# Second layer's hyena filter chain moved from the first token mixer to the first layer's last four experts

## The chip, the core and the metric

The kernel runs on one core of a Trainium2 chip. The metric is device time in microseconds (us) of one launch. Engines are called by the names of the profile: PE (TensorE matmuls), DVE (VectorE), ACT (ScalarE), POOL (GpSimd), SP (the queue that issues nearly all DMAs).

## What is computed

Two layers run over 256 context tokens and 256 latent tokens of width 1024. Each layer has a token mixer with four branches and then an expert-choice mixture of 16 experts. One of the branches is a Hyena long convolution. Its filters depend on weights alone, not on the tokens, so a layer's filters may be computed at any time before that layer's convolution:

```python
def hyena_filters(L, p):
    ...
    h = jnp.sin(p['hy_freq'][0] * (feats @ p['hy_w1'] + p['hy_b1']))
    h = jnp.sin(p['hy_freq'][1] * (h @ p['hy_w2'] + p['hy_b2']))
    h = (h @ p['hy_w3']).astype(jnp.float32)
    h = h * (jnp.exp(-dist[:, None] * jnp.abs(p['hy_decay'])) + HY_SHIFT)
    h = h / jnp.sum(jnp.abs(h), axis=0, keepdims=True)
    return h.reshape(L, HY_ORDER, HY_WIDTH)
```

The expert part reads 12 MB of weights per expert and layer (`w1`, `w3`, `w2`, each 1024x1024 in fp32) for 32 tokens per stream.

## The kernel before

The 256 filter positions are sines of sines. On the chip one layer's filters are a **chain** (`chain(l, hp)` inside `hyena_filters`): a 64x256 matmul, seven DVE operations that reduce the argument of the sine, a Sin on ACT, the same again, two 128x512 matmuls, a decay window (Abs, two Exp on ACT and a multiply-add on DVE), column sums by eight 128x1 matmuls, a reciprocal, four transposes, a scaling on DVE, and eight 128x512 matmuls with a DFT matrix `df`. The result is copied out of PSUM in four pieces (`A.activation(Hs[f](), p, AF.Copy)`) and each piece goes to DRAM with a DMA on SP (L775), where the layer's convolution fetches it much later with one DMA on POOL. The four pieces have a buffer each (`Hs`, four of them).

`hyena_filters` is called once, in the first layer's mixer, after the column blocks of GLA and before its `scan`. It runs `chain(0, ...)`, issues the loads of the second layer's small weights (`load_hy(1)`, L1749 to L1751), runs `chain(1, ...)`, and frees its memory. Everything of the chain lives in a region that is open for that time alone.

The mixer around it is a long row of PE work: column blocks (`pd`, tiles of 128x512), steps of the adaLN projection (`pa`, each waits for a 512 KB weight DMA), and the scan (`ps`, 64x64 products, level by level, with DVE and ACT work between levels).

`moe` comes after the mixer. `ffn(e)` takes eight 1 MB weight tiles for `w1` and `w3`, multiplies, applies Silu (ACT, L1636) and a product (DVE), transposes, takes four tiles of `w2`, multiplies, and copies out (`evac`, ACT L1687 and DVE L1685). Weight tiles sit in 19 slots; SP issues each when its slot is free and when the transfer eight places before it has landed, since eight completion semaphores are used in turn. Every four experts `gather` builds the tokens of the next group (`xg`, in the memory of `raws`) and `scatter` adds the last group's outputs (PE `pm`, DVE L1698). After expert 10 the last gather is done; `raws` and the transposed tokens `pre.xt` are then idle until the second layer's weights are reloaded at expert 15.

The order of instructions on each engine is fixed when the program is built, by a scheduler that may lift an instruction over others of its engine. Each engine, SP too, then works its row strictly in that order: an instruction that waits holds all behind it.

Of the kernel before, what the change touches and what calls it, by code (L numbers as in the profile page):

```python
# [51 lines left out]
HY = Pack()  # L52
# [301 lines left out]
def build(tc, ins, outT, dbg=None, stop=None):  # L354
# [66 lines left out]
    def early(name, off=0, **kw):  # L421
        o, c = C0.at[name]
        return c0(o + off, n=kw.pop("n", c - off), **kw)
# [298 lines left out]
    def hyena_filters(hps, df, rb):  # L722

        w, dec, h, ab = (rb.take(n) for n in (1024, 512, 1024, 1024))
        Hs = [rb.take(512) for _ in range(4)]
        def chain(l, hp):
            def hc(name, off=0, n=None, np_=64):
                o, c = HY.at[name]
                return hp(o + off, n=c if n is None else n, np_=np_)

            MAGIC = 12582912.0
            prev = early("feats", np_=33)
            for i, (wn, bn, fn, kdim) in enumerate((("w1", "b1", "f0", 33), ("w2", "b2", "f1", 64))):
                p = ps("s")
                mm(p[0:64, 0:256], hc(wn, np_=kdim), prev, True, True)
                a, k, g = (w(256 * q, n=256, np_=64) for q in (0, 1, 2 + i))
                V.tensor_scalar(a, p[0:64, 0:256], hc(bn), hc(fn), op0=OP.add, op1=OP.mult)
                V.tensor_scalar(k, a, 1.0 / (2 * math.pi), MAGIC, op0=OP.mult, op1=OP.add)
                V.tensor_scalar(k, k, MAGIC, None, op0=OP.subtract)
                c1 = 6.28125  # L740
                c2 = float(np.float32(2 * math.pi - c1))
                c3 = 2 * math.pi - c1 - c2
                for c in (c1, c2, c3):
                    V.scalar_tensor_tensor(a, k, -c, a, op0=OP.mult, op1=OP.add)
                V.tensor_scalar(a, a, 3.1415925, -3.1415925, op0=OP.min, op1=OP.max)
                A.activation(g, a, AF.Sin)
                prev = g
            A.activation(dec(), hp(HY.n, n=512), AF.Abs)
            pa = ps("s")
            for tb in range(2):  # L750
                p = ps("s")
                mm(p, w(768 + tb * 128, n=128, np_=64), hc("w3"), True, True)
# [4 lines left out]
            for q in range(4):  # L757
                for tb in range(2):
                    mm(pa[:, q:q + 1], ab(tb * 512 + q * 128, n=128), cs("ones", n=1), tb == 0, tb == 1)
# [1055 lines left out]
```

## Time and profile before

| | us |
|---|---|
| median of the runs | 1999.94 (1998.57 to 2007.31, three runs) |
| the profiled execution | 2006.5 |
| its span, first to last instruction | 2004.7 |
| PE busy | 1843.2 (92%) |
| DVE / ACT busy | 854.7 (43%) / 529.9 (26%) |

The page's picture in 40 slices of 50 us each shows the stages (a digit is the busy share in tenths, the last row GB/s moved by DMA):

```profile
PE   7999999999999899999897799999998999987877
DVE  5355658798743222221121345869865021110101
DMA  8641122364545999999999855333578999999999
GB/s 312 223 140 58 64 85 78 107 236 136 194 156 218 353 399 350 387 409 409 409 409 409 302 189 180 117 106 137 200 262 336 409 409 409 409 409 409 409 409 332
```

The first layer's mixer ends near 650 us, its experts near 1125 us, the second mixer near 1535 us; the rest is the second layer's experts. In the mixers PE is full and DMA is not; in the experts DMA stands at 409 GB/s for hundreds of us. The chain of the second layer lies between 71 and 121 us, in slices 2 and 3.

### The profile page before, as it was taken

The numbers are of one execution on the slowest core, as the hardware profiler recorded it, in microseconds if no ns is written. First come the engines' busy times: TensorE is split into PE (matmuls) and PEld (weight loads), VectorE is DVE, ScalarE is ACT, GpSimd is POOL, SyncE is SP. The second block draws the span as 40 slices with busy tenths as digits, with TensorE's granted clock in tenths as the row PEclk, the third lists the DMA queues.
The fourth block names the chain that finished last, engine by engine and source line by source line (L and its number), as shares of the span: only waits on it lengthen the run. The fifth ranks groups of instructions, "written<-read, shape, count | busy, mean of one in ns | idle before, by whom it ended". The sixth has DMA issues, their size and how long they took to land.

```text
span 2004.7 us, 28151 instructions
## 1 busy us (share of the span) xinstructions
PE 1843.2 (92%) x11524; PEld 1087.6 (54%) x11524; DVE 854.7 (43%) x1855; ACT 529.9 (26%) x932; POOL 27.9 (1%) x52
## 2 busy tenths in 40 slices
PE   7999999999999899999897799999998999987877
PEld 3667778877887443434232356788997333221213
DVE  5355658798743222221121345869865021110101
ACT  4433447522233110101000243447443000000000
POOL 0000000000000000000000010010000000000000
PEclk9989999999999899999999999999998999999999
DMA  8641122364545999999999855333578999999999
GB/s 312 223 140 58 64 85 78 107 236 136 194 156 218 353 399 350 387 409 409 409 409 409 302 189 180 117 106 137 200 262 336 409 409 409 409 409 409 409 409 332
DMA packets 154148, 550.07 MB, mean 274 GB/s; under 512 B 11042, under 2 KB 22690, under 8 KB 153124
## 3 DMA queue, kind: packets, MB, share of 16 engines
q1 hardware_dynamic: 153444, 545.13, 71.7%
q0 software_dynamic: 576, 3.15, 0.5%
q8 instruction: 91, 1.49, 0.3%
q14 instruction: 37, 0.30, 0.0%
HBM read 545.08 MB, written 3.15 MB: 273 GB/s over the span
## 4 chain that ended last, share of the span: by engine, by line
PE 69%; DMA 19%; DVE 7%; issue 3%; ACT 3%; SPq 0%; DVEq 0%; ACTq 0%
PE pd L431 40%; PE ps L431 15%; DMA base<-moe_w 8%; PE pm L431 7%; DMA r<-moe_w 6%; PE pa L431 4%; DMA base<-ada_w 2%; PE pm L428 1%; DMA base<-wg 1%; DVE base L527 1%; DVE r L844 1%; ACT r L843 1%; PE ps L1640 1%; DMA base<-cb 0%; DVE r L1236 0%
## 5 line engine op out<-in xcount | busy, mean ns | idle before, releaser
L431 PE MATMUL pd<-r 128*128 128x256 f32 (+3 forms) x2976 | 574.4, 364 | 12.9 <-DMA r<-moe_w 6.5
L431 PEld LDWEIGHTS pd<-r 128*128 128x128 f32 (+2 forms) x2976 | 427.3, 184 | 131.4 <-issue 53.8
L431 PE MATMUL pd<-r,r 128*128 128x512 f32 (+3 forms) x1304 | 282.6, 433 | 13.4 <-DMA r<-moe_w 10.8
L431 PEld LDWEIGHTS pd<-r,r 128*128 128x128 f32 (+2 forms) x1304 | 161.8, 166 | 105.0 <-issue 54.8
L844 DVE TENSOR_TENSOR r<-base,r 128x1024 fp32r<-128x1024 f32 x136 | 165.9, 1222 | 110.4 <-ACT r L843 110.0
L843 ACT ACTIVATE r<-base 128x1024 fp32r<-128x1024 f32 x136 | 143.4, 1058 | 252.2 <-PE pd L431 181.2
L431 PE MATMUL ps<-base 32*64 32x64 f32 (+12 forms) x2372 | 177.2, 279 | 15.1 <-DMA base<-hy 5.1
L431 PE MATMUL pd<-r,base 128*32 128x512 f32 (+1 forms) x680 | 166.5, 598 | 11.3 <-DMA r<-moe_w 10.6
L431 PEld LDWEIGHTS ps<-base 32*64 32x64 f32 (+7 forms) x2372 | 112.6, 142 | 76.3 <-issue 42.7
L431 PE MATMUL pm<-base 128*128 128x128 f32 (+12 forms) x660 | 106.1, 327 | 17.5 <-DVE base L1571 5.8
L431 PE MATMUL ps<-r,base 128*64 128x512 f32 (+4 forms) x468 | 98.6, 525 | 12.9 <-DVE base L1641 6.3
L431 PE MATMUL pd<-base 128*32 128x512 f32 (+1 forms) x408 | 100.5, 595 | 6.4 <-DMA base<-moe_w 5.6
L431 PEld LDWEIGHTS pm<-base 128*128 128x128 f32 (+5 forms) x660 | 72.8, 180 | 60.9 <-issue 33.6
L431 PEld LDWEIGHTS pd<-r,base 128*32 128x32 f32 (+1 forms) x680 | 42.0, 122 | 111.2 <-issue 76.4
L1637 DVE TENSOR_TENSOR r<-base,pd 64x512 f32<-64x512 f32 x16 | 10.9, 679 | 214.3 <-PE pd L431 214.3
L1637 DVE TENSOR_TENSOR base<-base,pd 128x512 f32<-128x512 f32 x16 | 11.0, 688 | 190.1 <-PE pd L431 155.9
L1636 ACT ACTIVATE base<-pd 128x512 f32<-128x512 f32 (+1 forms) x32 | 19.0, 594 | 251.1 <-PE pd L431 251.1
L431 PE MATMUL pa<-r,r 128*128 128x512 f32 (+1 forms) x384 | 82.4, 342 | 1.1 <-DVE base L905 1.1
L1687 ACT ACTIVATE base<-ps 32x512 f32<-32x512 f32 (+2 forms) x28 | 14.7, 525 | 251.6 <-PE ps L431 247.2
L1687 ACT ACTIVATE r<-ps 32x512 f32<-32x512 f32 (+2 forms) x32 | 15.3, 480 | 246.2 <-PE ps L431 240.3
L431 PE MATMUL pd<-base,r 128*32 128x512 f32 (+1 forms) x296 | 71.3, 597 | 9.3 <-DMA base<-moe_w 9.3
L1685 DVE COPY r<-ps 32x512 f32<-32x512 f32 (+2 forms) x32 | 17.8, 555 | 123.3 <-ACT r L1687 123.2
(246 smaller groups left out, 1728.8 us busy)
## 6 DMA issues: line engine op xcount, KB each, us to landing
r<-moe_w SPq DMA_DIRECT2D x251, 1024.0 KB, 18.1
base<-moe_w SPq DMA_DIRECT2D x131, 1024.0 KB, 17.4
base<-wg SPq DMA_DIRECT2D x152, 512.0 KB, 3.6
base<-ada_w SPq DMA_DIRECT2D x60, 512.0 KB, 4.7
base<-ada_t SPq DMA_DIRECT2D x24, 512.0 KB, 3.3
r<-ada_w SPq DMA_DIRECT2D x12, 512.0 KB, 10.2
base<-xT SPq DMA_DIRECT2D x4, 1024.0 KB, 6.8
filters<-r SPq DMA_DIRECT2D x8, 256.0 KB, 4.0
```

What stands on the lines that cost most here:

```text
L428: T.transpose(out, in_, ident)
L431: return T.matmul(out, lhsT, rhs, start=start, stop=stop, **kw)
L527: V.tensor_tensor_reduce(self.junk() if s == 0 else b(), b(), self.cb(s * 1024, n=1024), 1.0, cs("adab", l * 48 + c * 8 + j, n=1), OP.mult ...
L843: A.activation(w[0](), raw(), AF.Copy)
L844: V.tensor_tensor(w[1](), raw(), F(w[0]()), op=OP.subtract)
L1636: A.activation(s_(np_=rows), pa[0:rows, :], AF.Silu)
L1637: V.tensor_tensor(h_(np_=rows), s_(np_=rows), pb[0:rows, :], op=OP.mult)
L1640: T.transpose(p[:, q * rows:q * rows + rows], h_(q * 128, n=128, np_=rows), cs("ident", n=rows, np_=rows))
L1685: V.tensor_copy(dst, src)
L1687: A.activation(dst, src, AF.Copy)
```

## The change

`chain` becomes the whole of `hyena_filters(l, hp, c_, df, w, dec, h, ab, Hs)`, with its memory handed in. The first layer's call stays where it was. The second layer's call moves to the front of expert 12 of the first layer's `moe` (`next_filters`). There the working buffers are views of `pre.xt`, and the inputs (the small weights, the sine features `c_`, the DFT matrix `df`) are loaded anew into views of `raws`. Since `pre.xt` has no more room, there is one output buffer `Hs` instead of four.

```diff
-        chain(0, hps[0])
-        load_hy(1)
-        chain(1, hps[1])
...
+            A.activation(Hs[f % len(Hs)](), p, AF.Copy)
+            S.dma_start(out=Hd[l][:, f * 512:f * 512 + 512], in_=Hs[f % len(Hs)]())
...
+        def next_filters():
+
+            t, r = pre.xt, Buf(mem, raws[0].at, 3072)
+            hp, df, c_ = view(r, 0, HY.n + 1024), view(r, HY.n + 1024, 1024), view(r, HY.n + 2048, C0.n)
+            load_hy(1, hp)
+            S.dma_start(out=c_(n=258), in_=ins["c0"][:, 0:258])
+            S.dma_start(out=df(), in_=ins["df"][:, 0:1024])
+            hyena_filters(1, hp, c_, df, view(t, 0, 1024), view(t, 1024, 512), view(t, 1536, 1024), view(t, 2560, 1024),
+                          [view(t, 3584, 512)])
+
         nxt, spare = [], []
         gather(0)
         for gr in range(4):
             for j in range(4):
+                if not last and 4 * gr + j == 12:
+                    next_filters()
                 ffn(4 * gr + j)
...
-    hps = [mem.take(HY.n + 1024) for _ in range(2)]
+    hp0 = mem.take(HY.n + 1024)
...
+    def filters(r):
+        bs = [r.take(n) for n in (1024, 512, 1024, 1024)]
+        Hs = [r.take(512) for _ in range(4)]
+        hyena_filters(0, hp0, c0, df, *bs, Hs)
+        for b in bs + Hs + [hp0, df, c0]:
+            b.free()
```

Line numbers shift: the matmuls and the expert's weight DMAs are L431 and L1614 before, L431 and L1611 after; the store of a filter piece is L775 before and L778 after.

**SP between expert 11 and expert 13.** Before, the row from the last tiles of expert 11 holds weights alone:

```order
L1614 DMA r7_4871<-moe_w3 128x2x1024 x2
L1614 DMA r7_4871<-moe_w2 128x2x1024 x4
L1614 DMA r6_4867<-moe_w1 128x2x1024 x3
L1614 DMA base_58<-moe_w1 128x2x1024
L1614 DMA base_58<-moe_w3 128x2x1024 x3
L1614 DMA r7_4871<-moe_w3 128x2x1024
L1614 DMA r7_4871<-moe_w2 128x2x1024 x4
L1614 DMA r7_4871<-moe_w1 128x2x1024
```

After, it reads:

```order
L1611 DMA r7_4798<-moe_w2 128x2x1024 x4
L724 DMA base_58<-hy 64x644
L725 DMA base_58<-hyr 128x512
L726 DMA base_58<-hyr 1x512
L1729 DMA base_58<-c0 128x258
L1730 DMA base_58<-df 128x1024
L1611 DMA r6_4794<-moe_w1 128x2x1024 x3
L1611 DMA base_58<-moe_w1 128x2x1024
L1611 DMA base_58<-moe_w3 128x2x1024 x3
L1611 DMA r7_4798<-moe_w3 128x2x1024
L1611 DMA r7_4798<-moe_w2 128x2x1024
L778 DMA filters1_62<-base_58 128x512
```

Five loads have come in after expert 11's `w2`; nine weight tiles of expert 12 follow, then the first filter store. Behind that, the last three tiles of expert 12 and the other three stores stand in turn (tile, store, tile, store, tile, store), and only then the first tile of expert 13.

**PE at the scatter before expert 12 and in expert 12** (`pm` is the scatter; `pd422` and `pd423` are expert 12's `w1` and `w3`; `ps413` before is expert 11's `w2`, `ps412` to `ps421` after are the chain). Before:

```order
L431 MATMUL ps413_6225<-r7_4871,base_58 64x512 x16
L431 MATMUL pm414_6246<-r6_4867,base_58 128x256
L431 MATMUL pm415_6251<-r6_4867,base_58 128x256
L431 MATMUL pm414_6246<-r6_4867,base_58 128x256
L431 MATMUL pm415_6251<-r6_4867,base_58 128x256
L431 MATMUL pd422_6294<-r6_4867 64x512 x3
L431 MATMUL pm416_6256<-r6_4867,base_58 128x256 x2
L431 MATMUL pm417_6261<-r6_4867,base_58 128x256 x2
L431 MATMUL pd422_6294<-r6_4867 64x512 x2
```

After, from the second half of the scatter on (the first matmul of the chain, `ps412`, stands four scatter rows further ahead):

```order
L431 MATMUL pm409_6198<-r6_4794,base_58 128x256 x2
L431 MATMUL pm410_6203<-r6_4794,base_58 128x256 x2
L431 MATMUL pd422_6296<-r6_4794 64x512 x2
L431 MATMUL pm411_6208<-r6_4794,base_58 128x256 x2
L431 MATMUL pd422_6296<-r6_4794 64x512 x8
L431 MATMUL ps413_6228<-base_58 64x256
L431 MATMUL pd422_6296<-r6_4794 64x512
L431 MATMUL pd422_6296<-base_58,r6_4794 64x512 x4
L431 MATMUL ps415_6240<-base_58 128x512
L431 MATMUL ps416_6245<-base_58 128x512
L431 MATMUL pd423_6297<-base_58,r6_4794 64x512
L431 MATMUL ps414_6239<-base_58 128x1
```

The chain's matmuls have come in among those of the scatter and of expert 12; the last of them, `ps421`, stands behind the seventh of the sixteen matmuls of `w3`.

**PE in the first mixer.** Before, between the end of the first chain (`ps26`) and the scan (`ps37`, `ps38`, ...), the second chain (`ps27` to `ps36`) is spread over column blocks and projection steps; its first part reads:

```order
L431 MATMUL ps26_596<-r4_530,base_58 128x512 x2
L431 MATMUL ps27_604<-base_58 64x256
L431 MATMUL pa45_762<-base_58 32x256 x8
L431 MATMUL pd78_1153<-r2_227,r3_231 128x512 x13
L431 MATMUL pa45_762<-base_58 32x256 x4
L431 MATMUL pd78_1153<-r2_227,r3_231 128x512 x8
L431 MATMUL ps28_614<-r4_530,base_58 64x256
```

After, the scan (`ps27`, `ps28`, ...) follows the first chain at once, and the same column block (now `pd68`) stands between its levels:

```order
L431 MATMUL ps26_596<-r4_530,base_58 128x512 x2
L431 MATMUL ps27_607<-base_58 64x64 x8
L431 MATMUL ps28_617<-base_58 64x64 x8
L431 MATMUL pa35_689<-base_58 32x256
L431 MATMUL ps29_627<-base_58 64x64 x8
L431 MATMUL ps30_637<-base_58 64x64 x8
```

The column blocks that stood beside the second chain now stand in the scan and after it; the expert slots have the same number and places in memory as before.

## Rows read from the trace of the kernel before

**Rows 1.** Windows: us, busy us of each engine, PE clock, DMA share, GB/s.

```profile
300.00:400.00 100.00, 99.70 (x514) 79.83 (x514) 82.75 (x220) 64.80 (x133) 0.69 (x1) 1.00 0.26 90
85.00:119.20 34.20, 30.73 (x145) 17.71 (x144) 12.46 (x24) 8.73 (x13) 0.31 (x1) 0.90 0.55 178
119.00:158.00 39.00, 37.22 (x653) 27.30 (x652) 29.83 (x61) 14.20 (x28) 2.17 (x4) 0.94 0.39 124
1000.00:1050.00 50.00, 45.72 (x200) 17.26 (x198) 11.02 (x22) 3.54 (x6) 0.31 (x1) 1.00 1.03 409
1050.00:1100.00 50.00, 38.03 (x166) 10.55 (x164) 4.27 (x7) 2.36 (x4) 0.00 (x0) 1.00 1.03 409
```

**Rows 2.** Timeline of PE, 85 to 119 us: start, us, what, idle before.

```profile
85.14 0.64 PE L431 MATMUL ps<-base 33*64 33x256 f32 x2
...
92.88 0.64 PE L431 MATMUL ps<-r,base 64*64 64x256 f32 x2
...
97.30 0.64 PE L431 MATMUL pa<-base 128*32 128x256 f32 x8 [1.38 <-DMA base<-ada_w]
...
99.69 1.98 PE L431 MATMUL ps<-base,r 64*128 64x512 f32 x4
...
102.50 0.28 PE L431 MATMUL ps<-base,r 128*128 128x1 f32 x2
104.03 0.64 PE L431 MATMUL pa<-base 128*32 128x256 f32 x8 [1.25 <-DMA base<-ada_w]
...
105.17 2.37 PE L431 MATMUL ps<-base,r 128*128 128x1 f32 x14
...
109.26 1.05 PE L428 MATMUL ps<-base,r 128*128 128x128 f32 x4
...
111.82 7.45 PE L431 MATMUL ps<-r,base 128*128 128x512 f32 x16
```

**Rows 3.** Timeline of DVE in the same stretch, the second chain.

```profile
93.56 0.53 DVE L737 TENSOR_SCALAR r<-ps,base 64x256 f32<-64x256 f32 x1 [3.46 <-PE ps L431]
...
96.13 0.29 DVE L745 TENSOR_SCALAR r<-r 64x256 f32<-64x256 f32 x1
100.84 0.69 DVE L755 SCALAR_TENSOR_TENSOR r<-r,ps 128x512 f32<-128x512 f32 x1 [4.43 <-PE ps L431]
...
110.42 1.28 DVE L768 TENSOR_TENSOR r<-r,ps 128x512 f32<-128x512 f32 x2 [2.20 <-PE ps L428]
...
112.76 0.67 DVE L769 TENSOR_TENSOR r<-r,base 1x512 f32<-1x512 f32 x1
```

**Rows 4.** Timeline of ACT: a table load, an Abs and a filter copy of the chain.

```profile
74.48 1.28 ACT L754 ACT_TABLE_LOAD   x1
...
102.48 0.63 ACT L756 ACTIVATE r<-r 128x512 f32<-128x512 f32 x1 [0.23 <-DVE r L755]
...
115.87 0.60 ACT L774 ACTIVATE r<-ps 128x512 f32<-128x512 f32 x1 [9.49 <-PE ps L431]
```

**Rows 5.** Timeline of SP at the second chain's four stores.

```profile
116.49 4.43 SPq L775 DMA_DIRECT2D filters<-r  x4
```

**Rows 6.** The page's DMA issues: KB each, median us from issue to landing.

```profile
r<-moe_w SPq DMA_DIRECT2D x251, 1024.0 KB, 18.1
```

**Rows 7.** Timeline of PE at the end of expert 11 and in expert 13.

```profile
994.90 1.94 PE L431 MATMUL pd<-r,base 128*64 128x512 f32 x8 [0.61 <-DMA r<-moe_w]
...
1005.14 1.94 PE L431 MATMUL ps<-r,base 128*64 128x512 f32 x8 [0.63 <-DMA r<-moe_w]
1007.76 1.99 PE L431 MATMUL pm<-r,base 128*128 128x256 f32 x8 [0.68 <-ACT base L1687]
...
1046.07 1.94 PE L431 MATMUL pd<-r 128*64 128x512 f32 x8 [0.62 <-DMA r<-moe_w]
```

**Rows 8.** Timeline of DVE: the last four of the sixteen scatter operations.

```profile
1018.58 1.74 DVE L1698 SCALAR_TENSOR_TENSOR base<-pm,base 128x256 f32<-128x256 f32 x4 [1.19 <-PE pm L431]
```

**Rows 9.** The stores of the filters (L775) by source line.

```profile
DMA to landing us min/median/max: 2.3/4.0/6.3
```

More of the change, by code (lines that the diff above doesn't have):

```diff
@@ L419, in sp, with early @@
         return sm(o + off, dims, **kw)
-    def early(name, off=0, **kw):
+    def early(b, name, off=0, **kw):
         o, c = C0.at[name]
-        return c0(o + off, n=kw.pop("n", c - off), **kw)
+        return b(o + off, n=kw.pop("n", c - off), **kw)
     ident = cs("ident")
@@ L719, in split @@
         V.tensor_tensor(lo, src, F(hi), op=OP.subtract)
[L722 to L749, printed above, removed]
-            for tb in range(2):
-                p = ps("s")
-                mm(p, w(768 + tb * 128, n=128, np_=64), hc("w3"), True, True)
-                ht, at = h(tb * 512, n=512), ab(tb * 512, n=512)
-                A.activation(at, dec(), AF.Exp, scale=early("ndist", tb, n=1))
-                V.scalar_tensor_tensor(ht, at, 0.05, p, op0=OP.add, op1=OP.mult)
-                A.activation(at, ht, AF.Abs)
-            for q in range(4):
-                for tb in range(2):
-                    mm(pa[:, q:q + 1], ab(tb * 512 + q * 128, n=128), cs("ones", n=1), tb == 0, tb == 1)
-            rec = mem.take(4)
-            V.reciprocal(rec(n=4), pa[:, 0:4])
-            V.tensor_copy(dec(0, [[128, 4], [1, 128]]), rec(0, [[1, 4], [0, 128]]))
-            rec.free()
-            pa = ps("s")
-            for q in range(4):
-                tr(pa[:, q * 128:q * 128 + 128], dec(q * 128, n=128))
-            for tb in range(2):
-                V.tensor_tensor(h(tb * 512, n=512), h(tb * 512, n=512), pa, op=OP.mult)
-            V.tensor_tensor(h(512, n=512, np_=1), h(512, n=512, np_=1), hp(HY.n + 512, n=512, np_=1), op=OP.add)
-            for f in range(4):
-                p = ps("s")
-                for tb in range(2):
-                    mm(p, df(tb * 512 + f * 128, n=128), h(tb * 512, n=512), tb == 0, tb == 1)
-                A.activation(Hs[f](), p, AF.Copy)
-                S.dma_start(out=Hd[l][:, f * 512:f * 512 + 512], in_=Hs[f]())
-        chain(0, hps[0])
-        load_hy(1)
-        chain(1, hps[1])
-        for b in hps + [df, w, dec, h, ab] + Hs:
-            b.free()
@@ L1740, in moe @@
         return nxt if nxt else (None, None)
-    hps = [mem.take(HY.n + 1024) for _ in range(2)]
+    hp0 = mem.take(HY.n + 1024)
     df = mem.take(1024)
     half = CN.at["ind64"][0]
-    def load_hy(l):
-        r = ins["hyr"][l]
-        S.dma_start(out=hps[l](n=HY.n, np_=64), in_=ins["hy"][l])
-        S.dma_start(out=hps[l](HY.n, n=512), in_=bass.AP(tensor=r.tensor, offset=r.offset, ap=[[0, 128], [1, 512]]))
-        S.dma_start(out=hps[l](HY.n + 512, n=512, np_=1), in_=r[1:2, :])
-    load_hy(0)
+    load_hy(0, hp0)
     S.dma_start(out=cn(n=half), in_=ins["cn"][:, :half])
```

51 lines of the change are left out of this document (50 added, 1 removed).

## Prediction

> **What bounds the kernel now.** I read the windows by stage first. In the first mixer PE is the bound: 99.70 of 100 us busy from 300 to 400 us, with DMA at 90 GB/s [rows 1]. Where the second layer's chain now runs, PE is a little less full: 30.73 of 34.2 us from 85 to 119 us, so 3.5 us idle, at a mean clock of 0.90 of its upper level [rows 1]. The last experts of the first layer are the opposite: DMA stands at 409 GB/s from 1000 us on, and PE is busy 38.03 of 50 us from 1050 to 1100 [rows 1]. The timeline of PE there shows the same from the other side: each group of eight matmul records waits for its weight tile to land [rows 7]. A tile of 1024 KB at 409 GB/s takes 2.56 us, and from issue to landing it takes 18.1 us [rows 6], so seven tiles are on the way at any time. So the change takes work from a place where PE time is what counts and puts it where PE, DVE and ACT have time to spare but a microsecond of idle DMA moves the end of the stage by a microsecond. Everything after that stage starts later by the same amount: the second layer reuses its memory, and nothing there is waiting for a fixed time. The layout and number of weight slots are the same, so nothing else in the expert stage differs.
>
> **What the front gains.** The second chain's PE work is 0.64 + 0.64 (the two small matmuls), 1.98 (two 64x512), 0.28 + 2.37 (eight column sums), 1.05 (four transposes) and 7.45 (eight DFT matmuls), together 14.4 us [rows 2]. All of it lies on a PE that is otherwise full, so it goes from the path whole if the rest of PE's row stays as dense as it is. The 3.5 us of idle PE in that window come mostly from projection steps that wait for their weight DMA (1.38 and 1.25 us are two of them [rows 2]). Those steps don't vanish, they move into the scan; there the steps stand further apart, so I count about half of the idle as gained, 2 us. Against this, the column blocks and steps that filled PE beside the chain now have to fit into the scan and behind it. The scan before ran with 37.22 of 39 us busy [rows 1], so its gaps take no more than they took; the order of after puts about as much filling between its levels as before, and the rest behind it, where PE was full. I take **16.5 us** for the front. The upper end is 14.4 + 3.5 and the slow clock: 34.2 us at 0.90 instead of 1.00 are 3.4 us of lost work, so 21 us. The lower end is 10 us, if the filling leaves new gaps in the scan and the reshuffled row of the mixer costs some, an estimate from 14.4 less two and a half times the scan's present idle of 1.8 us. DVE and ACT lose some 9 us of work each in the front; neither is full in that window (12.46 and 8.73 of 34.2 us [rows 1]), so I count nothing for it.
>
> **What expert 12 pays: bytes.** The new loads are 64x644, 128x512, 1x512, 128x258 and 128x1024 words of 4 bytes, 1.09 MB, and the four stores 1.05 MB. On a DMA that is full, 2.13 MB at 409 GB/s cost 5.2 us. Before, the same bytes moved in the mixer, where DMA was at 178 GB/s [rows 1], for nothing.
>
> **What expert 12 pays: SP's row.** SP works in order. The first of the five loads waits until expert 11's `w3` has left the memory of `raws`, which is at 994.90 + 1.94 us in the time of before [rows 7]. Before, SP had by then issued four tiles of expert 12. But expert 11's four `w2` tiles are in flight and land until 1005.1 [rows 7], so DMA stays full. Then come the five loads, 2.65 us, and nine tiles of expert 12, 23.1 us: DMA has work until 1005.1 + 2.65 + 23.1 = **1030.9**. The next in SP's row is the first filter store, which waits for the chain. Until it is issued, no weight is.
>
> So the question is when the chain ends. Its loads land behind the last `w2` tile, at about 1006. Its first matmul stands behind the scatter's first tiles on PE, which started at 1007.8 [rows 7]: about 1010. On DVE the argument reduction is mixed with the sixteen scatter operations, of which the last four ended at 1018.58 + 1.74 = 1020.3 before [rows 8]. The copies that the scatter needs now stand on ACT behind the chain's Abs and a table load of 1.28 us [rows 4], so I add 1 us: first Sin at about 1021.5. The second matmul stands behind eight matmuls of expert 12's `w1`, two tiles at 1.94 us [rows 7]: 1025 at the latest, 1024 taken. The second reduction takes 93.56 to 96.42 us before [rows 3], 2.9 us: 1027; the second Sin stands on ACT behind expert 12's Silu: 1027.5. From there the chain is serial: two matmuls 1.98, DVE 0.69, Abs 0.63, column sums 2.65, reciprocal and copy about 0.6 (an estimate, it lies between the rows), transposes 1.05, scaling 1.28, bias row 0.67, the last two of the first DFT group 2 x 0.93, copy 0.60 [rows 2 to 4]: 12.0 us, and half a microsecond for expert 12's matmuls in between. First store at **1040**. As a check, from the first matmul to the first store it took 85.14 to 116.49 us before, 31.4 [rows 2, 5]; here it is 30. So DMA runs dry for some 9 us.
>
> Then there is one output buffer: copy two waits until store one has landed, and so on. A hop is one landing plus a copy and its signals, 0.8 us. Stores landed in 2.3 to 6.3 us before, median 4.0 [rows 9]. Here at most one weight tile is in flight ahead of a store, so I take a value near the lower end, 2.6, and a hop of 3.4: three hops, last store at 1050.2. Only one weight tile goes with each hop. Expert 13's first tile is issued at 1050.6; with the store's 0.64 us, its own 2.56 and the fixed part of a landing (2.3 less 0.64, so 1.7) it lands at 1055.5 and the fourth at 1063.2. Before, the fourth tile was there at 1046.07 [rows 7]. The stage ends **17 us** later. In terms of DMA time that is 5.2 us of bytes, 9 us dry, and 3 us lost between the stores. The upper end is 28 us, with hops of 7.1 (6.3 + 0.8). The lower end is 9 us: the chain done before 1031, bytes and store gaps alone.
>
> The row on landings gives 2.3 to 6.3 us for 256 KB [rows 9]. The Trainium skill (DMA: Bandwidth & Descriptors, Anatomy of one DMA) puts a fixed cost of about 2.0 us on every DMA, mostly for the completion, to which the bytes come on top. By that page a store of 0.64 us would land in 2.64 us on an empty queue and the three hops would cost 10.3 us; by the median row they would cost 14.4 us and the stage 21.
>
> **The sum.** 17 - 16.5 = +0.5 us on the profiled execution's 2006.5. That execution lies 0.3% above the median of the runs, 1999.94, and I carry the difference over to the median: **2000.5 us**. Differences under 0.5%, some 10 us, are about what a measurement of this kernel can't tell from no change.
>
> **The rivals.** (1) Faster: the chain hides. If DVE and ACT, nearly idle in expert 12 (4.27 and 2.36 of 50 us are busy a little later [rows 1]), get through the chain in 20 us instead of 30, the first store is ready while weights are still in flight and SP hardly waits. Then the loss is 9 us, and with a front gain of 19 the time is 1990. For it speaks how little else these engines do there; against it that the chain's steps depend on each other and that its matmuls stand in a row with expert 12's. (2) Slower: the single buffer decides. Each store must land before the next copy, and SP holds the weights behind each. If the landings are as long as the longest of before, 6.3 us, because each store queues behind a weight tile and then waits for its write to be acknowledged, the loss is 28 us and the time 2011; from a landing of 5.5 us on it is beyond 10 us. For it speaks the spread of 2.3 to 6.3; against it that the queue is nearly empty. (3) The front gives little: PE's time in the mixer is only reshuffled, with new gaps in the scan where DVE is at 29.83 of 39 us [rows 1]. With a gain of 10 the time is 2007, still within the same band. That the change doesn't do what it says is out: the order shows the second chain gone from the mixer and standing at expert 12.
>
> **How the numbers follow.** The forecast, the two sides cancel within 10 us, 0.56 (with rival 3 in it); the chain hides or the front gives over 20, 0.21; the stores or a longer chain cost more, 0.23. The forecast's own range is 1991 to 2010. To hold 8 in 10 the range reaches half into both rivals: 1986 to 2014.
>
> **What would show it.** In the trace of after, the scan should begin right after the first chain's end near 85 us, and the mixer's end (the gap of PE near 650 us) should come about 16 us earlier. At expert 12 the windows should show DMA under 409 GB/s for some 20 us, with SP's first filter store 30 us after the chain's first matmul and the next three 3 to 4 us apart; expert 13's fourth tile should land within 3 us of where it did before (17 later from that stage, 16.5 earlier from the front). Wrong would be the front if the mixer's end moves by less than 10 us; wrong would be the expert side if DMA has no dry stretch, or one of over 15 us.

## The result: slower by 1.3 per cent

| | us |
|---|---|
| before, median | 2001.47 (1998.57 to 2007.31, four runs) |
| after, median | 2029.46 (2023.23 to 2032.02, four runs) |
| ratio | 1.0127, 95% interval 1.0100 to 1.0153 |
| forecast | 2000.5, range 1986 to 2014 |
| profiled execution, before and after | 2006.5 and 2031.7 (spans 2004.7 and 2029.9) |

The ratio is an estimate from all the runs; the two medians alone give 1.014. The forecast was wrong in size: it had the two sides cancel, at +0.5 us. To see where the 25.2 us between the two profiled executions lie, five instructions that both traces have are laid side by side:

| mark | before | after | shift | this stage |
|---|---|---|---|---|
| a DVE operation near 300 us, in the attention branch (L1215, now L1212) | 300.84 | 289.92 | -10.9 | -10.9 |
| first Silu of expert 0 (its table load on ACT) | 673.48 | 672.75 | -0.7 | +10.2 |
| first scatter operation behind expert 11 (DVE) | 1009.81 | 1009.43 | -0.4 | +0.3 |
| first operation of the last scatter, behind expert 15 | 1128.95 | 1151.27 | +22.3 | +22.7 |
| end of the span | 2004.7 | 2029.9 | +25.2 | +2.9 |

So the front gave 10.9 us and not 16.5, experts 12 to 15 cost 22.7 and not 17, and the rest of the first mixer took back 10.2 us that the prediction does not have at all. The windows of after, in the stretches and columns of [rows 1]:

```profile
85.00:119.20 34.20, 34.06 (x506) 23.01 (x506) 20.60 (x40) 7.28 (x14) 0.00 (x0) 0.60 0.41 132
119.00:158.00 39.00, 38.23 (x356) 27.37 (x351) 16.80 (x31) 16.30 (x30) 2.13 (x5) 0.96 0.40 137
300.00:400.00 100.00, 90.02 (x439) 71.14 (x438) 88.26 (x218) 59.13 (x121) 0.69 (x1) 0.93 0.37 129
1000.00:1050.00 50.00, 45.41 (x170) 18.40 (x166) 17.82 (x40) 11.46 (x16) 0.31 (x1) 0.97 0.76 280
```

Three of the four rows carry one cost each; the second shows that PE is no less full in the rest of the scan than before (38.23 of 39 us, before 37.22). In the first, PE has no idle time left, but the granted clock is 0.60 where it was 0.90. In the third PE, which was full, is idle for 10 of 100 us. In the fourth, DMA moves 280 GB/s instead of 409.

The last stage, closer, on SP's timeline of after (start, us, what, idle before), then what SP waited for there (us in total, times, longest), the landing times of these stores (the trace has two of the four), and DMA from 1000 to 1060 us in slices of 1.5 us:

```profile
1009.03 6.36 SPq L1611 DMA_DIRECT2D r<-moe_w  x2
1040.44 0.34 SPq L778 DMA_DIRECT2D filters<-base  x1
1040.87 0.38 SPq L1611 DMA_DIRECT2D r<-moe_w  x1
1044.47 0.34 SPq L778 DMA_DIRECT2D filters<-base  x1
...
1049.20 0.34 SPq L778 DMA_DIRECT2D filters<-base  x1
...
1054.26 0.34 SPq L778 DMA_DIRECT2D filters<-base  x1
1054.69 2.08 SPq L1611 DMA_DIRECT2D r<-moe_w  x4
```

```profile
SPq L778 <- ACT base L777: 36.1, 4, 25.0
```

```profile
DMA to landing us min/median/max: 3.3/3.7/4.0
```

```profile
GB/s 415 318 291 289 410 404 410 410 410 410 407 407 415 410 410 410 410 407 410 213 36 0 0 0 5 0 11 176 253 268 354 212 262 322 270 366 190 257 214 336
```

SP stands for 25.0 us before the first store; DMA empties at about 1029.5 and stays so until 1040.4. Then come three hops of 4.0, 4.7 and 5.1 us with one weight tile each. On PE's timeline the answer to [rows 7] is this; the first of the three is the last group of expert 12, the next two are the first and the fourth tile of expert 13:

```profile
1056.73 1.94 PE L431 MATMUL ps<-r,base 128*64 128x512 f32 x8 [0.53 <-DMA r<-moe_w]
1061.36 1.94 PE L431 MATMUL pd<-r,r 128*64 128x512 f32 x8 [2.68 <-DMA r<-moe_w]
...
1069.00 1.94 PE L431 MATMUL pd<-r 128*64 128x512 f32 x8 [0.62 <-DMA r<-moe_w]
```

### The profile page after: what moved, and what is told of

It reads as the page before. It is cut to its first block, busy times and chain, and to the rows that moved or that the text cites. A ratio compares the mean times of both kernels' runs of the same rounds, so it can differ in the third digit from the quotient of the medians.

```text
span 2029.9 us, 28145 instructions
## 1 busy us (share of the span) xinstructions
PE 1858.6 (92%) x11524; PEld 1093.8 (54%) x11524; DVE 855.5 (42%) x1855; ACT 534.1 (26%) x934; POOL 27.3 (1%) x52
## 2 busy tenths in 40 slices
DMA packets 154436, 550.72 MB, mean 271 GB/s; under 512 B 11074, under 2 KB 22850, under 8 KB 153412
## 4 chain that ended last, share of the span: by engine, by line
PE 71%; DMA 18%; DVE 6%; ACT 3%; issue 2%; SPq 0%; DVEq 0%; ACTq 0%
PE pd L431 41%; PE ps L431 15%; DMA r<-moe_w 9%; PE pm L431 7%; DMA base<-moe_w 6%; PE pa L431 5%; DMA base<-ada_w 2%; PE pm L428 2%; DMA base<-wg 1%; ACT r L840 1%; DVE r L841 1%; PE ps L1637 1%; DMA base<-xT 0%; DVE r L1233 0%; DVE base L527 0%
## 5 line engine op out<-in xcount | busy, mean ns | idle before, releaser
L431 PE MATMUL pd<-r 128*128 128x256 f32 (+3 forms) x2976 | 568.7, 362 | 12.5 <-DMA r<-moe_w 8.0
L431 PEld LDWEIGHTS pd<-r 128*128 128x128 f32 (+2 forms) x2976 | 426.2, 184 | 129.5 <-issue 51.2
L431 PE MATMUL pd<-r,r 128*128 128x512 f32 (+3 forms) x1304 | 286.2, 437 | 15.0 <-DMA r<-moe_w 12.4
L431 PEld LDWEIGHTS pd<-r,r 128*128 128x128 f32 (+2 forms) x1304 | 164.3, 168 | 110.9 <-issue 57.5
L431 PE MATMUL ps<-base 32*64 32x64 f32 (+14 forms) x2410 | 193.7, 292 | 16.6 <-DMA base<-hy 4.8
L431 PE MATMUL pd<-r,base 128*32 128x512 f32 (+1 forms) x680 | 166.7, 598 | 11.3 <-DMA r<-moe_w 9.7
L431 PEld LDWEIGHTS ps<-base 32*64 32x64 f32 (+7 forms) x2410 | 123.4, 154 | 86.7 <-issue 47.7
L431 PE MATMUL pm<-base 128*128 128x128 f32 (+12 forms) x660 | 106.1, 327 | 17.8 <-DVE base L1568 5.8
L431 PE MATMUL pd<-base 128*32 128x512 f32 (+1 forms) x408 | 100.5, 595 | 6.4 <-DMA base<-moe_w 5.6
L431 PEld LDWEIGHTS pm<-base 128*128 128x128 f32 (+5 forms) x660 | 72.8, 180 | 61.3 <-issue 32.7
L431 PE MATMUL ps<-r,base 128*64 128x512 f32 (+4 forms) x450 | 91.2, 523 | 15.7 <-ACT r L749 4.9
L431 PEld LDWEIGHTS pd<-r,base 128*32 128x32 f32 (+1 forms) x680 | 42.0, 122 | 111.2 <-issue 74.6
L1634 DVE TENSOR_TENSOR r<-base,pd 64x512 f32<-64x512 f32 x16 | 10.9, 679 | 213.8 <-PE pd L431 213.8
L431 PE MATMUL pa<-r,r 128*128 128x512 f32 (+1 forms) x384 | 83.6, 347 | 1.2 <-DVE base L902 1.1
L431 PE MATMUL pd<-base,r 128*32 128x512 f32 (+1 forms) x296 | 74.7, 606 | 9.3 <-DMA base<-moe_w 9.3
## 6 DMA issues: line engine op xcount, KB each, us to landing
r<-ada_w SPq DMA_DIRECT2D x12, 512.0 KB, 10.2
```

What stands on the lines that cost most here:

```text
L431: return T.matmul(out, lhsT, rhs, start=start, stop=stop, **kw)
L1634: V.tensor_tensor(h_(np_=rows), s_(np_=rows), pb[0:rows, :], op=OP.mult)
```

## The experiments

In the table, **front** is the shift of the mark near 300 us against 300.84, and **experts** the time from the first scatter operation behind expert 11 to the first one behind expert 15, less 119.1 (119.14 in the kernel before, 119.00 and 119.05 in the two kernels without the chain). Both are read from one profiled execution of each kernel. How far one execution can be trusted: warm (below), which has no chain at expert 12 either, gives -1.3 in the experts column, and the front column moves by several us between kernels whose front is the same, for a reason that comes out below. The ratio is against runs of the kernel before on the same chip, whose medians lay between 2005.3 and 2008.7 (2001.47 for after).

| run | what differs | ratio (interval) | front | experts |
|---|---|---|---|---|
| after | | 1.0127 (1.0100 to 1.0153) | -10.9 | 22.7 |
| hold | after, old layout | 1.0080 (1.0052 to 1.0108) | -8.2 | 24.7 |
| no_chain_new | after, no second chain | 0.9993 (0.9975 to 1.0011) | -8.0 | 0 |
| no_chain_old | hold, no second chain | 0.9940 (0.9917 to 0.9962) | -8.3 | 0 |
| both | before, and the chain at expert 12 | 1.0089 (1.0065 to 1.0113) | 0.1 | 23.5 |
| oneact | hold, stores on ACT's queue | 1.0054 (1.0037 to 1.0072) | -7.4 | 14.3 |
| four2 | hold, four output buffers | 1.0051 (1.0025 to 1.0076) | -12.0 | 19.3 |
| fouract2 | both of these | 1.0022 (1.0002 to 1.0042) | -7.9 | 9.0 |
| split | fouract2, chain in three parts | 0.9992 (0.9966 to 1.0018) | -11.6 | 6.0 |
| loads | no_chain_old, and the five loads | 0.9977 (0.9959 to 0.9996) | -14.6 | 2.8 |

### Three costs apart: the layout, the front, the experts

In the order of PE's instructions, after and before differ at the two places that the change names, and besides in some 250 records between 300 and 450 us, which it does not touch. The memory of this kernel is handed out by a first-come allocator. `hps[1]`, 1668 columns, is no longer taken, so later buffers of the first layer lie elsewhere. The run **hold** takes these columns again, frees everything in the old order, and writes nothing there:

```diff
-    hp0 = mem.take(HY.n + 1024)
+    hp0, hold = mem.take(HY.n + 1024), mem.take(HY.n + 1024)
...
-        for b in bs + Hs + [hp0, df, c0]:
+        for b in [hp0, hold, df] + bs + Hs + [c0]:
```

> The changed kernel with one thing more: a dummy buffer of 1668 columns is taken where the second parameter buffer stood and freed where it was freed, so that every later buffer of the first layer lies where it lay before the change. Nothing is written to it. Theory (layout): the changed kernel lost 12.4 us between 310 and 450 us because buffers taken later lie elsewhere, other pairs of work share memory, and the scheduler orders the attention's products and the merges of layer 1 differently; with the old layout the 11 us won in the front last to the first experts. Time near 2017 (12 below the changed kernel, 0.6 per cent), and the first Silu of expert 0 near 662 against 673.5 before. Rival (the chain's own work kept the chip warm or filled a gap, so that its absence costs the attention stage something whatever the order): time as the changed kernel, 2029, first Silu near 673.

> The changed kernel without the chain at expert 12: the second chain is left out altogether, and layer 2 reads layer 1's filter, so the output is not the reference's. It shows the front half of the change by itself, with the new layout. Theory (layout): minus 11 in the front, plus 12.4 in the attention and merge stage, nothing at expert 12: 2003 to 2005, about as the kernel before, and the second mixer as before. Rival (the loss at expert 12 is not the chain's but carried there from the stage before): still 10 or more above the kernel before.

> The second chain left out (layer 2 reads layer 1's filter, so the output is not the reference's) and the dummy buffer kept, so that layer 1's buffers lie as before the change. It measures what leaving the second chain out of the first mixer is worth by itself. Theory (layout): the gain of 11 us at 300 us lasts to the end: 1988 to 1992. The prediction's own term was 16.5 (1984). Rival: the attention stage gives it back also in this layout, 2001 to 2004.

The two runs without the chain leave out `next_filters()` and let the second layer fetch `Hd[0]`. The first Silu of expert 0 came at 664.75 in hold and 664.55 in no_chain_old, at 672.75 in after and 675.7 in no_chain_new: in the old layout the front's gain lasts, in the new one 10.2 us go in both kernels. In times of whole runs the layout is 0.47% (after against hold, on two chips) and 0.53% (the two runs without the chain), 9 to 11 us. Where they go, from 300 to 400 us: the windows of hold and of after, then PE's merge products in hold and after, then what PE waited for in after from 300 to 450 us:

```profile
300.00:400.00 100.00, 99.71 (x513) 80.92 (x512) 84.27 (x207) 60.73 (x124) 0.69 (x1) 1.00 0.32 108
```

```profile
L431 PE MATMUL pd<-r 128*128 128x512 f32 x192 | 49.6, 398 | 0.0
```

```profile
L431 PE MATMUL pd<-r 128*128 128x512 f32 x136 | 36.1, 402 | 0.0
```

```profile
PE pm L428 <- DVE base L541: 3.7, 1, 3.7
PE ps L431 <- ACT base L1258: 3.4, 6, 1.1
PE pm L428 <- DVE base L1273: 1.5, 1, 1.5
PE ps L431 <- ACT base L1249: 1.0, 2, 0.7
```

These are the products by which the mixer merges its branches. In the old order 192 records of them lay in this stretch, between the attention's own products, and gave PE work while ACT and DVE computed the softmax; in the new one there are 136. PE's waits on these four lines of ACT and DVE are new (of the four, hold has 0.2 us on L1273 alone), and its clock falls to 0.93. The cause, a layout that changes the scheduler's order, is shown by hold: nothing else differs, and PE's order from 300 to 450 us is that of before again, where 254 records lie otherwise in after; which buffer's new place made the scheduler move which product was not traced.

**both** is the kernel before with its second chain kept, and the chain computed again at expert 12:

```diff
         hyena_filters(0, hp0, c0, df, *bs, Hs)
+        load_hy(1, hold)
+        hyena_filters(1, hold, c0, df, *bs, Hs)
```

> The kernel before, with the second chain still in the first mixer and computed again, from the same loads, ahead of expert 12 as in the changed kernel. It measures the expert half by itself. Theory: the 22 to 24 us that the trace of the changed kernel shows between expert 11 and the scatter before the third group are the half's own cost and do not depend on the front: 2022 to 2026, with the four stores of expert 12 4 to 5 us apart and DMA nearly still just before the first one. The prediction's term was 17 (2018). Rival (part of it comes from the front's shift or the layout): 2012 to 2017.

Experts 12 to 15 cost 23.5 us there: the half has its price wherever the front stands. The whole time, 0.9% or 18 us, lies between the range named and the rival's, within what the medians scatter; the experts column is what decides.

### What the experts pay for

Two suspects were taken apart: the one output buffer, and SP's row, in which expert 13's weights stand behind the stores.

```diff
-            S.dma_start(out=Hd[l][:, f * 512:f * 512 + 512], in_=Hs[f % len(Hs)]())
+            (S if l == 0 else A).dma_start(out=Hd[l][:, f * 512:f * 512 + 512], in_=Hs[f % len(Hs)]())
...
-                          [view(t, 3584, 512)])
+                          [view(t, o, 512) for o in (3584, 0, 2560, 3072)])
```

The first edit alone is oneact, the second alone four2, both together fouract2.

> The kernel with the old layout (the run called hold) and four output buffers for the four filters at expert 12 instead of one: the parts of the same free memory that the chain no longer reads by then. The stores stay in SP's row. Theory (SP's row is what costs): the hops between the stores go (the four copies follow PE's products 1.8 us apart, so the last store is issued near 1037 instead of 1046.1 on hold's clock), but SP still stands before the first store from 1007 to 1032 with expert 13's weights behind it: 8 to 10 us less than hold, that is 7 above the kernel before. Rival (the single buffer's hops are the bulk of the half's 25 us): 15 or more less than hold.  Rival (stores land late whatever the buffers): as hold.

> The run called hold with one thing changed: the four stores at expert 12 are issued from ScalarE's queue instead of SP's. One output buffer as in the changed kernel, so the hops remain (4 to 6 us each), but nothing of expert 13's weights stands behind them. Theory (SP's row): DMA keeps moving weights through 1020 to 1040, expert 13 starts within 8 us of no_chain_old, and of the half's 25 us about 7 remain (2.1 MB more at about 410 GB/s are 5.2): 17 to 19 less than hold, 1 or 2 below the kernel before. Rival (the hops decide): 0 to 5 less than hold.

> Both: old layout, four output buffers, and the stores on ScalarE's queue. Theory (SP's row): the same as oneact within 3 us, since with nothing behind the stores their spacing costs nothing; 17 to 20 less than hold, 1 to 4 below the kernel before. Rival (the hops decide): as four. If both matter apart, it is faster than either by 5 or more.

> The run called four with its buffers put right: there the third and fourth of the four lay on the filter's own taps, so the last products had to wait for the copies and read overwritten values. Here the four are the chain's free part, the first third of the layers' buffer and the two halves of the absolute values, none of which is read by then. Stores in SP's row. Theory (two causes apart: hops, and SP's row ahead of the first store): the hops are gone, SP still stands from about 1005 to the first store: of the 25 us between no_chain_old and hold 14 to 17 remain, 5 to 8 above the kernel before. Rival: the hops were all, 5 to 10 remain.

> The run called fouract with the same mended buffers: stores on ScalarE's queue, four buffers. Expert 12's own products still stand behind the chain's in PE's row, so in fouract expert 13 began 15 us later than in no_chain_old, and DMA thinned to 150 to 315 GB/s for 8 us since its slots were not freed. Theory: 10 us of the 25 remain: 1 or 2 above the kernel before (front 8.5). Rival (SP's row was the whole loss): 5 remain, 3 or 4 below the kernel before.

In four and fouract the third and fourth buffers lay on the filter's taps (`view(t, 1536, 512)` and the next), which the products still to come read: their last filters are not the reference's, and these products waited for the copies. They measured 1.0055 (experts 18.6) and 1.0007 (experts 8.5); four2 and fouract2, with the buffers put right, say nearly the same. In terms of the experts column the two causes add: 24.7 with neither edit, 5.4 less with four buffers, 10.4 less with ACT's queue, 15.7 less with both. Both gains were misjudged: oneact left 14.3 where about 7 were expected, or 20 and more by the rival, and four2 left 19.3 where 14 to 17 were expected. The whole times, on three chips, bear out the sum and not the shares: oneact lies 0.26%, four2 0.29% and fouract2 0.58% below hold, each known to about 0.3%. In oneact the hops remain and get longer (landings of 3.1 to 6.9 us), and cost what they cost on SP's queue: 5.3 us (14.3 less 9.0), against 5.4.

The Trainium skill (DMA: Bandwidth & Descriptors, Issuing engines are not separate DMA queues) says that issuing from several engines saves only the time that a sequencer takes to initiate a DMA, which is small. That holds for the transfers: the same bytes moved. But oneact against hold is 10.4 us in the experts column, and the reason is in the same page's section on the anatomy of one DMA: waits happen on the issuing sequencer, so what stands behind a waiting DMA is not even queued.

9.0 us remained, more than the bytes. The stores are off SP's row by then, but SP's weights still waited for them. What SP waited for in oneact from 1000 to 1085 us (its longest item), in fouract2 from 1025 to 1040 (all of it), and in split (the next run) from 985 to 1130 (this item):

```profile
SPq L1611 <- DMA filters<-base: 30.7, 4, 10.5
```

```profile
SPq L1611 <- DMA filters<-base: 11.3, 2, 10.7
SPq L1611 <- PE ps L431: 0.3, 1, 0.3
SPq L1611 <- PE pd L431: 0.2, 1, 0.2
```

```profile
SPq L1613 <- DMA filters<-base: 14.3, 4, 6.9
```

The eight completion semaphores are used in turn by the transfers of both queues, so the weight eight places behind a store goes out only when that store has landed, on whichever queue it stands. In fouract2 SP issued a weight at 1021.69 and the next at 1032.78, just after the first store had landed; four weights then went out within 2.3 us, so their slots had been free before. That is where DMA thins out to 168 GB/s, and why the hops still cost something in oneact, where DMA falls to 11 GB/s. The expectation of fouract2 put the thin stretch down to slots that expert 12 frees late; SP's waits do not show that, and as far as they go the chain's place in PE's row matters here in that it sets when the first store is ready. **split** makes `hyena_filters` a generator with two stops, and `moe` takes one part ahead of each of experts 12, 13 and 14:

```diff
+        yield
         pa = ps("s")
...
+        yield
         for f in range(4):
...
-                if not last and 4 * gr + j == 12:
-                    next_filters()
+                if not last and gr == 3:
+                    if j == 0:
+                        chain = next_filters()
+                    next(chain, None)
```

> The run called fouract2 with the chain cut into three parts that stand ahead of expert 12 (loads and the two sine layers), 13 (taps, norm) and 14 (the products of the DFT and the stores): in PE's row each part's products stand between those of an expert whose inputs are there, and expert 12's no longer behind the whole chain. Theory (PE's row is the third cause): what remains of the 25 us is the bytes, 2.1 MB at 410 GB/s, 5.2 us, and 1 or 2 for the thin stretch around the five loads: 6 to 8, so 1 to 3 below the kernel before, and DMA never under 250 GB/s between 1000 and 1080. Rival (the chain's use of ACT and DVE, not PE's row, holds the experts): as fouract2, or later.

> The run called no_chain_old with the five loads of the chain ahead of expert 12 and nothing else of it: no chain, no stores, layer 2 reads layer 1's filter, so the output is not the reference's. It prices the loads by themselves: 1.1 MB at 410 GB/s are 2.7 us, and the stretch of five small loads in which DMA moved 270 to 360 GB/s for 5 us adds about 1. Theory: 3 to 5 us above no_chain_old, 4 to 6 below the kernel before. Rival (SP's waits for the memory of the gathers cost more): 8 or more above no_chain_old, with SP standing still ahead of the first load.

DMA from 1000 to 1060 us, in slices of 1.5 us, of fouract2 and of split:

```profile
GB/s 412 407 410 415 401 412 412 407 415 404 410 415 401 412 410 410 410 410 410 287 259 206 168 186 238 422 419 415 426 426 412 418 407 401 418 404 412 410 401 421
```

```profile
GB/s 415 407 410 410 410 410 410 407 415 407 410 410 410 410 410 404 418 404 407 407 407 415 410 401 412 396 418 407 410 407 407 412 412 401 418 410 407 396 407 421
```

Split has no dip there. Its stores come from 1058 to 1068 us, SP's waits for them are shorter, and DMA stays at 350 GB/s or more around them. Its 6.0 us are the bytes' 5.2 and little more. In the experts column loads puts 2.8 of them on the five loads, whose bytes are 2.7; by whole times it lies 0.37%, or 7 us, above no_chain_old, on another chip. So the 24.7 us of hold are 15.7 for the stores in SP's row and the hops, of which the row is about two thirds, 3.0 for the chain in one piece, and 6.0 that are nearly all bytes. That the 3.0 come from SP's wait for the first store is read from the trace: split moves PE's row and the stores together, so it does not tell the two apart.

### Why the front gave less than 16.5

In the scan, groups of 64 records of 32-row products are the same in all kernels. On PE's timeline of after, and of warm (below):

```profile
95.10 2.79 PE L431 MATMUL ps<-base 32*64 32x64 f32 x64
...
112.29 2.78 PE L431 MATMUL ps<-base 32*64 32x64 f32 x64
115.00 2.93 PE L431 MATMUL pd<-r,r 128*128 128x512 f32 x6
117.86 1.91 PE L431 MATMUL ps<-base 32*64 32x64 f32 x64
```

```profile
114.87 1.90 PE L431 MATMUL ps<-base 32*64 32x64 f32 x64
```

2.78 against 1.90 us is the clock: it falls from 1.00 to 0.50 (1.2 GHz instead of 2.4) within about 10 us of the scan's beginning, in all eleven traces with the new front and nothing added to the scan, and stays there for 20 to 34 us in nine of them. In before the scan's clock fell too, but was back within 10 us. What it costs, from windows of 85 to 185 us of before, after, no_chain_old and loads (the columns as above):

```profile
85.00:185.00 100.00, 94.75 (x1109) 66.67 (x1109) 52.67 (x107) 32.80 (x59) 2.79 (x6) 0.93 0.39 125
```

```profile
85.00:185.00 100.00, 99.09 (x1224) 72.11 (x1223) 54.16 (x106) 32.32 (x59) 3.33 (x7) 0.85 0.35 120
```

```profile
85.00:185.00 100.00, 99.20 (x1187) 72.05 (x1185) 53.15 (x103) 31.48 (x57) 2.65 (x7) 0.81 0.35 115
```

```profile
85.00:185.00 100.00, 98.10 (x1234) 72.18 (x1222) 57.12 (x111) 32.60 (x60) 3.40 (x7) 0.88 0.37 120
```

After: 14.4 us of PE work gone, 4.3 us of idle gone (99.09 less 94.75), and 8 us lost to a clock of 0.85 instead of 0.93: 10.7, measured 10.9. For no_chain_old it is 14.4 + 4.5 - 12 = 6.9, measured 8.3. The terms of 8 and 12 are estimates that take all of PE's work as slowed in the clock's ratio; the groups of 64 took 1.46 times as long at half the clock, not twice.

The runs hold a better test than these sums. In the eleven traces PE works the same records in the same order up to the mark near 300 us, and still the mark comes 7.4 to 14.6 us early. It goes with the clock of this window: 7.4 to 8.3 us in the five traces at 0.81 (hold, no_chain_new, no_chain_old, oneact, fouract2), 9.3 to 12.0 in the three at 0.85 or 0.86 (after, four, four2), 11.6 to 14.6 in the three at 0.88 (split, fouract, loads). A line through the eleven gives 16 us at the 0.93 of before, an estimate that lies outside of what they cover. Whether the clock follows what PE works on was tried by giving PE some products on constants in the scan, which nothing reads:

```diff
+                if l == 0 and dk == 32 and lev == 1:
+                    p = ps("s")
+                    for i in range(16):
+                        mm(p, ident, cn(CN.at["ident"][0], n=512), i == 0, i == 15)
                 ada_bg.run(SCN[l])
```

> The run called no_chain_old (second chain left out, layer 2 reads layer 1's filter, so the output is not the reference's) with 16 products of 128 by 128 by 512 on constants added after the third level of the first scan, near 100 us; nothing reads their result. In no_chain_old the granted clock is 0.50 from 90 to 120 us, and one group of 64 products of 32 rows takes 2.78 us there, against 1.90 at clock 1.00 in the kernel before. Theory (the clock's level there is what the front gain is short of, and it depends on what PE is given): the 16 products cost 7.5 us at the high clock, and bring the clock back to 1.00 for the rest of the scan, the groups of 64 behind them take 1.90, and the 300 us mark stands within 3 us of no_chain_old's in spite of them. Rival (the scan's own chain, not the clock, sets the stretch, or the clock stays low whatever PE gets): the 300 us mark 7 to 15 us later, groups of 64 at 2.78.

> The run called split with 4 products of 128 by 128 by 512 on constants after the third level of the first scan, whose result nothing reads. In warm the 16 products took 14.9 us (32 records of 0.47), not the 7.5 its expectation counted, and the 300 us mark came only 2.9 us later, so the clock gave back 12. Theory (a few such products are enough to bring the clock back to its upper level): 3.7 us spent, up to 10 won, the 300 us mark 3 to 6 us earlier than in split, the whole 5 to 8 us below the kernel before. Rival (it takes more work than 4 products): clock stays at 0.50 until after 115 us, as split or 4 later.

> The same 4 products one level of the scan earlier, ahead of where the clock fell in split. Theory (a few are enough, and the earlier the more is won): at least as early as split_w4 at the 300 us mark. Rival (the clock falls only behind them, since what follows is the same row of 32-row products): as split plus 2 to 4.

> The same with 8 products after the third level. Theory (4 are enough): 3 to 4 us later than split_w4 at the 300 us mark. Rival (4 are too few, 8 bring the clock back): earlier than split_w4, 0 to 3 us earlier than split.

| run | added to | ratio (interval) | front |
|---|---|---|---|
| warm, 16 products | no_chain_old | 1.0016 (1.0002 to 1.0031) | -5.4 |
| split_w4, 4 products | split | 0.9998 (0.9982 to 1.0014) | -12.9 |
| split_w4_early, 4, one level earlier | split | 0.9993 (0.9977 to 1.0008) | -13.5 |
| split_w8, 8 products | split | 1.0022 (1.0004 to 1.0041) | -12.0 |

The 16 products of warm, in two records each, took PE 15.5 us (the group by line from 93 to 114 us):

```profile
L431 PE MATMUL ps<-base 128*128 128x512 f32 x32 | 15.5, 645 | 0.0
```

Still the mark near 300 us came only 2.9 us later than in no_chain_old, and 2.0 later than the latest of the eleven: the clock was 1.00 from 100 us on, and gave most of the difference back. Behind the 16 products of warm and the 8 of split_w8 it did not fall again before 430 us; in each of the eleven traces without such products it did. The four of split_w4 show nothing of the kind. The clock was back at 1.00 from 95 us on, ahead of the first of them at 97.4:

```profile
95.00:100.00 5.00, 5.00 (x73) 3.14 (x72) 3.32 (x8) 0.63 (x1) 0.00 (x0) 1.00 0.51 189
```

It fell again between 105 and 110 us, and so it did in split_w4_early, where the four came during the first fall. The fronts of the three versions of split lie within the 7.4 to 14.6 of the traces with nothing added, and the times expected of them did not come: split_w4 was to be 3 to 6 us earlier than split at the mark and was 1.3 earlier, split_w8 3 to 4 later than split_w4 and was 0.9 later. So that the front's 16.5 was about right at the clock that the prediction assumed rests on the eleven traces, not on these runs. No version of the three is measurably faster than the kernel before or than split; split_w8 is slower than before by 0.2%.

## Why the prediction was wrong, step by step

- **Front, 16.5 us: mis-sized, 10.9.** The work of 14.4 was right, and of idle 4.3 us went where 2 were counted. The step that failed took PE's time as a sum of durations at the old clock. The text even counted a clock of 0.90 as something to win, up to 3.4 us; in the stretch of [rows 1] the clock fell to 0.60, and from 85 to 185 us it took some 8. The lower bound of 10 was made for new gaps in the scan. There were none: PE was busy 34.06 of 34.20 us. That the 10.9 lies inside the stated 10 to 21 is luck: in the ten other traces with this front and nothing added to the scan the gain was 7.4 to 14.6, as the clock came out.
- **"The reshuffled row of the mixer costs some": the step that was missing.** The text let the 14.4 us go "whole if the rest of PE's row stays as dense as it is", and looked at the scan, where the change moves instructions, but not at 300 to 450 us; it put the reshuffled row at nothing in the sum. In this stage 10.2 us went, by the layout, and with the old layout (hold) they did not. Of the 24.7 us between the forecast's sum and the measured 25.2 this is the largest part; 5.6 are the front, 5.7 the experts. The order of PE's row shows the difference before any run. Rival 3 had the right result, a front that gives little, by another mechanism. The test named, a mixer's end that moves by less than 10 us, came out as the text says a wrong front would: 0.7.
- **Expert 12, when the first store goes out: right.** DMA had work until 1029.5 (1030.9 forecast), and the first store went out at 1040.44 (1040 in the time of before, from which after differs by 0.4 there). The dry stretch was about 11 us, against 9, as it began earlier. From its first matmul, at 1009.75, to the first store the chain took 30.7 us, where the text had 30: it did not hide, as rival 1 had it.
- **The hops: mis-sized.** 4.0, 4.7 and 5.1 us against 3.4 each, 3.6 us in all. The text took a landing of 2.6, near the lower end of [rows 9], as the queue would be nearly empty ahead of a store; the two landings that the trace has are 3.3 and 4.0, and copy and signals took 0.7. What the step left out is the weight tile that SP issues 0.4 us behind each store and that moves beside it. In four2 the first two stores, with no weight behind them, landed in 2.3 us, and the third, with one 0.4 us behind it, in 3.6. So the 2.64 that the text worked out from the Trainium skill (DMA: Bandwidth & Descriptors, Anatomy of one DMA, whose figure was measured on DMAs that GpSimd issues) comes near a store by itself, and the median row's 4.0 one with a tile behind it: the three hops took 13.8 us, where the median row gave 14.4 and the page 10.3.
- **From the last store to expert 13's first tile: mis-sized**, 7.1 us against 5.3. With the hops (3.6) and the first store (0.4) this makes 5.8, and the experts' cost exceeds the forecast's 17 by 5.7.
- **Bytes, 5.2 us: right.** Split leaves 6.0, and loads 2.8 for its 2.7. Only the text's "the same bytes moved in the mixer" is not quite so: `c0` and `df` are loaded a second time, and the kernel moves 0.65 MB more than before (550.72 MB against 550.07).
- **Rival 2, the single buffer, was half right.** The experts' 22.7 lay within its 28, but the buffer was worth 5.4 us and the stores' place in SP's row 10.4. The forecast's own working had the latter (9 dry and 3 between the stores). By the text's own sum the rival passes 10 us from a landing of 5.8 on, not 5.5.
- **The sum.** -16.5 + 17 became -10.9 + 10.2 + 0.3 + 22.7. The remaining 2.9 us lie behind the last scatter. Fourteen of the fifteen other traces show 2 to 7 us between the last two marks too, both among them, whose front is the old one, so they look like the one trace of before rather than like the change; that was not settled.

## What to carry to other kernels

Moving a step changes what is taken from memory and when; where a scheduler works by the buffers' places, compare the order far from the moved step as well, and hold the old places with a dummy buffer to see what the layout alone does. A DMA that waits for a computation should not stand in the row that feeds the weights: another queue gave 10.4 us here and more buffers 5.4, by one trace each. Another queue is not enough while both queues' transfers take completion semaphores in turn from one set: look at what SP waits for after the move as well. Spreading the computation over three experts brought its price down to little more than its bytes. A single trace's stage can hide a clock that comes out otherwise the next time; compare the stage over all traces that share its instructions. Time taken from a full PE comes back only at the clock that the row left behind is granted.

## What the runs showed of the chip

- PE with 0.14 us of idle time in 34.2 was granted 0.50 of its clock for 27 us (after), in a row of 32-row products with a few larger ones between. The same row of records was granted 0.81 to 0.88 from 85 to 185 us in eleven traces, and the mark behind it moved by 7 us. The Trainium skill (TensorE: Matmul & The Clock Gate, Part 1) lets the clock follow how busy PE has been; the busy share of the records does not tell it here (34.06 of 34.20 us at 0.60). With 8 or 16 products of 128 rows and 512 columns added (split_w8, warm), the clock rose during them and stayed at 1.00 until 430 us; with four it fell again.
- A 256 KB store landed after 2.3 us with no weight beside it (four2), 3.3 to 4.0 with a 1 MB load issued behind it (after), and 6.1 to 7.5 among weights (split, DMA at 350 to 421 GB/s), where it cost little.
- A store on ACT's queue held weights on SP's for up to 10.7 us (fouract2), as this program gives both queues' transfers their completion semaphores from one set of eight.
